# All three mixer gates as seven half-sized products with tokens as the stationary side, in a decoder layer on one core

## The chip, the core and the metric

One core of a Trainium2 chip runs the whole kernel as one program. A core has a matrix engine (TensorE, PE in the profile, its weight loads PEld), a vector engine (VectorE, DVE), a scalar engine (ScalarE, ACT), GpSimd (POOL), a queue engine that issues transfers (SyncE, SP), and 16 DMA engines that all queues share. Each engine works through its own queue in order; semaphores hold an instruction until what it needs is there. The metric is device time in microseconds (us), lower is better.

## What is computed

One layer of a hybrid decoder on 512 tokens of width 1024. The part that matters here is the mixer:

```python
proj = x @ w_in
(da_q, da_k, da_v, sb_q, sb_k, sb_v, dl_q, dl_k, dl_v, gates) = jnp.split(proj, _split_points(), axis=-1)
...
g = jax.nn.sigmoid(gates).reshape(B, S, N_BRANCHES, D)
merged = (g[:, :, 0] * (o_da @ w_branch_da) + g[:, :, 1] * (o_sb @ w_branch_sb)
          + g[:, :, 2] * (o_dl @ w_branch_dil))
return merged @ w_out
```

`o_da`, `o_sb` and `o_dl` are the outputs of differential attention (4 heads), stick-breaking attention (8 heads) and dilated attention (4 heads in 3 groups); each is 512 tokens by 512. The three gates are 512 by 1024 each, so their weights are 1024 by 1024. Behind the mixer come a layer norm, a squared-ReLU MLP, a second sigmoid gate on an embedding, and a second layer norm.

All values are float32. A product is made in three passes of a reduced-precision format: an operand is split into a high part (a cast, on ACT) and a low part (the subtraction, on DVE), and high x high, high x low and low x high add up in PSUM. So each 128x128 block of a product costs three matmuls, and each weight tile costs one cast and one subtraction of 1024 columns.

## The kernel before, in words

The program is a list of *items* made ahead of time; an item is a run of matmuls into one PSUM bank, with an evacuation behind it. The main loop (L1783) goes through the list. For each item it splits the weights that it needs and some ahead, evacuates the item before, takes a step of the attention work, and issues the item's matmuls. A plain input tile (`t_item`, L258) takes another step halfway. A scheduler then orders each engine's instructions by a model of time, so an engine's order is near the program's but not the same.

**Weights.** `load` and `fill` (L165) put 512 KB transfers on SP's queue into seven raw buffers; `split_next` (L200) splits a chunk into one of six pairs of buffers for high and low parts. Weights are thus split up to six chunks, and loaded up to thirteen, ahead of their use.

**Attention.** Each head (or, for differential attention, each head and block of 128 queries) is a generator whose steps are taken by `step` (L1754), started in a fixed order, eight stick-breaking heads, four dilated heads, sixteen differential blocks, under a budget of PSUM banks. Its matmuls, exponentials and copies fall between the items. The order of the input projections is written out in `main_order` (L36): the last ones are the q and k tiles of differential attention, with its value projection after the second head, and eight plain tiles of gate 1.

**Seven products.** Several large products are made by a scheme with seven half-sized products in place of eight (halves of the contraction, tokens and columns), with sums of operand blocks on both sides and sums of the results. The token side is formed once by `mixer_forms` (L515) from a second copy of x that POOL's queue reloads (`load_xr`, L330); products are numbered 1 to 7 after their token form. The weight sums are made in one of two ways: by DVE in the kernel's buffers, or by transfers that copy and accumulate from DRAM to DRAM on POOL's queue (`sum_steps`, L905), eight 512 KB steps per group of four sums, four groups in turn, so many steps per item (`RATES`, L1777). A step waits for a recent subtraction on DVE, so that the transfers spread over the main stream, and for the steps of its own group that it reads.

**Gates and branches.** Gate 1 is eight plain tiles (128 output columns stationary, 512 tokens moving, 24 matmuls each). Gates 2 and 0 are eight *pairs* of column tiles (`gate_pair`, L570), each seven products with a 128-column weight form stationary and 256 tokens moving, 84 matmuls 256 wide. Their weight sums are made by DVE: four additions of 512 columns per pair. Branch tiles (`branch_item`, L545; 12 matmuls 512 wide, weights stationary) are placed between the parts of the pairs. `gate_sig` (L503) applies the sigmoid, behind the last exponential of attention. Products and merged rows have channels on partitions, so the merged tiles are split and used directly as the stationary side of the output projection (`wout_items`, L724).

The value projection of two dilated groups (`value_pair`, L401) and the gate after the mixer (`pleg_items`, L813) are seven-product stages of the other shape: a token form of 128 tokens stationary, 512 weight columns moving, 7 x 2 halves x 12 matmuls.

The lines that pace all this before:

```python
        RATES = 1.8, 1.0
        ...
            if 12 <= n < wout_at - 6:
                credit += it["size"] * (RATES[0] if n < pairs_at[0] else RATES[1])
            elif n > wout_at + 22:
                credit += 1 / 3
```

Of the kernel before, what the change touches and what calls it, by code (L numbers as in the profile page):

```python
# [10 lines left out]
F32 = mybir.dt.float32  # L11
# [24 lines left out]
def main_order():  # L36


    o = [("T", "sb_q", 0), ("T", "sb_k", 0), ("T", "sb_q", 1), ("T", "sb_k", 1), ("V", "sb_v", 0)]
    for j in (2, 3):  # L40
        o += [("T", "sb_q", j), ("T", "sb_k", j)]
    for h in range(4):
        for g in range(3):
            o += [("T", "dl_q", 4 * g + h), ("T", "dl_k", 4 * g + h)]
            if h == 1 and g == 0:
                o += [("V", "dl_v", g)]
        if h == 2:
            o += [("V", "dl_v", 1), ("V", "dl_v", 2)]
    for h in range(4):
        o += [("T", "da_q", h), ("T", "da_k", h)]  # L50
        if h == 1:
            o += [("V", "da_v", 0)]
    for j in range(8):
        o += [("T", "gate", 8 + j)]
    return o


def trunk(tc, a, out):
    nc = tc.nc
    es = ExitStack()  # L60
    with es:
# [210 lines left out]
        def t_evac(name, j):  # L272
            def ev(ps):
# [5 lines left out]
                elif name == "gate":  # L279
                    t = slot("graw")  # L280
                    cp(t, ps)
                    gate_raw[j] = (t, 1.0)
# [199 lines left out]
        for kind, name, j in order[2:]:  # L482
            if kind == "T":
                if name == "gate":
                    continue
# [17 lines left out]
        def gate_sig(i, j):  # L503
            t, sign = gate_raw.pop(8 * i + j)

            with tc.issue_after(last_exp[0]):
                nc.scalar.activation(t, t, AF.Sigmoid, scale=sign)
            sg[i, j] = t
# [36 lines left out]
        def branch_item(i, j):  # L545
            if j % 2 == 0:
                branch_chunk[i] = chunk(a["wb"][i, j // 2].rearrange("p j k m -> p (j k m)"), 1024)
            c = branch_chunk[i]

            def mm(ps):  # L550
                for k in range(4):
                    s = slice(((j % 2) * 4 + k) * P, ((j % 2) * 4 + k) * P + P)
                    h, lo = oTs[4 * i + k]
                    mm3(ps, c["h"][:, s], c["l"][:, s], h, lo, k == 0, k == 3)

            def ev(ps):
                gate_sig(i, j)
                g = sg.pop((i, j))
                nc.vector.tensor_mul(g, g, ps)
                if i == 1:  # L560
                    merged[j] = g
                else:
                    nc.vector.tensor_add(merged[j], merged[j], g)
                if i == 0:
                    merged[j] = split(merged[j], "m")
            item([c] if j % 2 else [], mm, ev, need=[c], size=0.5)

        branch_chunk = {}

        def gate_pair(n, between):  # L570

            i, q = (2, 0)[n // 4], n % 4
            wa, wb = [load(a["wgp"][n, m].rearrange("p b k n -> p (b k n)"), 1024) for m in range(2)]
            ws = load(None, 1024)
            lo, up = slice(0, 512), slice(512, 1024)
            cs = {}
            b = {}

            def first_sums():
                nc.vector.tensor_add(ws["raw"][:, lo], wa["raw"][:, lo], wb["raw"][:, up])  # L580
                nc.vector.tensor_add(ws["raw"][:, up], wb["raw"][:, lo], wb["raw"][:, up])

            def second_sum():
                nc.vector.tensor_add(wb["raw"][:, up], ws["raw"][:, up], wa["raw"][:, lo])

            def third_sum():
                nc.vector.tensor_add(wa["raw"][:, up], wb["raw"][:, up], wa["raw"][:, up])

            def prod(ps, p, start, stop):
                c, o = cs[p]  # L590
                for k in range(4):
                    s = slice(o + k * P, o + k * P + P)
                    mm3(ps, c["h"][:, s], c["l"][:, s], *xf[p][k], start and k == 0, stop and k == 3)

            def bank(name):
                def f():
                    b[name] = at_bank()
                    return b[name]
                return f

            def part_a():
                c = part_of(wa, 0, 1024)
                cs[1], cs[2] = (c, 0), (c, 512)

                def mm(ps):
                    prod(ps[:, HC], 2, True, True)
                    b["s"] = slot("up")
                    nc.scalar.copy(b["s"][:, HB], ps[:, HC])
                    prod(ps[:, HB], 1, True, False)

                def ev(ps):
                    b[0], b[1] = slot("graw"), slot("graw")
                    gate_raw[8 * i + 2 * q], gate_raw[8 * i + 2 * q + 1] = (b[0], 1.0), (b[1], -1.0)
                    nc.vector.tensor_add(b[0][:, HB], ps[:, HB], b["s"][:, HB])
                item([c], mm, ev, need=[c], bank=bank("x"), size=0.5)

            def part_b():
                c3 = part_of(ws, 0, 1024, first_sums, (wa, wb))
                c4 = part_of(wb, 0, 1024, second_sum, (wa, ws))
                cs[7], cs[5], cs[4], cs[6] = (c3, 0), (c3, 512), (c4, 0), (c4, 512)  # L620

                def mm(ps):
                    prod(ps[:, HB], 7, True, False)
                    prod(b["x"][:, HB], 6, False, False)

                def ev(ps):
                    nc.scalar.copy(b["s"][:, HC], b["x"][:, HB])
                    nc.scalar.copy(b["s"][:, HB], ps[:, HB])
                item([], mm, ev, need=[c3, c4], bank=bank("y"), size=0.5)

            def part_c():
                c5 = part_of(wa, 512, 512, third_sum, (wb,))
                cs[3] = (c5, 0)

                def mm(ps):
                    prod(ps[:, HB], 5, False, False)

                def ev(ps):
                    nc.vector.tensor_add(b[1][:, HC], ps[:, HB], b["s"][:, HB])
                item([cs[5][0]], mm, ev, need=[cs[5][0]], bank=lambda: b["x"], size=0.25)  # L640

            def part_e():
                need = [cs[3][0], cs[4][0]]

                def mm(ps):
                    prod(b["x"][:, HB], 3, False, True)
                    prod(ps[:, HB], 4, False, True)

                def ev(ps):
                    nc.vector.tensor_add(b[1][:, HB], ps[:, HB], b["s"][:, HC])  # L650
                    nc.scalar.copy(b[0][:, HC], b["x"][:, HB])
                item(need, mm, ev, need=need, bank=lambda: b["y"], size=0.5)
            part_a()
            for t in between[:2]:
                branch_item(*t)
            part_b()
            for t in between[2:]:
                branch_item(*t)
# [1317 lines left out]
```

## Time and profile before

| | |
|---|---|
| median of three runs | 1056.42 us (1056.42 to 1056.5) |
| span of the profiled execution | 1054.8 us |
| granted TensorE clock | 0.997 |
| instructions | 15599 |

By the trace, the eight plain gate tiles start after the last q and k tiles of differential attention; the gate pairs begin at 479.55 us, the output projection at 629.98 and the embedding gate's products at 688. In the profile, a row of a group names the line, engine, operation, output and inputs with shapes and the count, then the busy time and the mean duration of one, and last the idle time of that engine before them with what ended it. Matmuls are pipelined and their ends are modelled, so a matmul's duration is longer than the time until the next one starts. A row of windows gives the busy time of each engine in a stretch of the span.

### The profile page before, as it was taken

The numbers are of one execution on the slowest core, as the hardware profiler recorded it, in microseconds if no ns is written. First come the engines' busy times: TensorE is split into PE (matmuls) and PEld (weight loads), VectorE is DVE, ScalarE is ACT, GpSimd is POOL, SyncE is SP. The second block draws the span as 40 slices with busy tenths as digits, with TensorE's granted clock in tenths as the row PEclk, the third lists the DMA queues.
The fourth block names the chain that finished last, engine by engine and source line by source line (L and its number), as shares of the span: only waits on it lengthen the run. The fifth ranks groups of instructions, "written<-read, shape, count | busy, mean of one in ns | idle before, by whom it ended". The sixth has DMA issues, their size and how long they took to land.

```text
span 1054.8 us, 15599 instructions
## 1 busy us (share of the span) xinstructions
PE 1044.2 (99%) x5802; PEld 902.9 (86%) x5802; DVE 775.2 (73%) x1386; ACT 571.2 (54%) x994; POOL 145.4 (14%) x223
## 2 busy tenths in 40 slices
PE   9999999999999999999999999999999999999996
PEld 6887788889888888889898988888999889889885
DVE  6888667768764757769768773888777877877966
ACT  6666545536442545547544452685656665666651
POOL 0002401221211102231111130100101100000000
PEclk9999999999999999999999999999999999999998
DMA  8346776976997719872666693258888868777502
GB/s 318 113 151 223 169 208 173 300 271 165 325 310 210 222 39 290 230 240 94 220 173 213 162 334 104 65 160 277 237 298 263 238 243 274 242 236 237 192 34 80
DMA packets 63261, 219.75 MB, mean 208 GB/s; under 512 B 7913, under 2 KB 8825, under 8 KB 63185
## 3 DMA queue, kind: packets, MB, share of 16 engines
q1 hardware_dynamic: 37056, 126.80, 34.6%
q0 software_dynamic: 25552, 91.04, 32.9%
q8 instruction: 45, 0.74, 0.3%
q10 hardware_dynamic: 576, 0.92, 0.2%
q14 instruction: 32, 0.25, 0.1%
HBM read 216.61 MB, written 81.81 MB: 283 GB/s over the span
## 4 chain that ended last, share of the span: by engine, by line
PE 96%; DVE 2%; DMA 0%; ACT 0%; issue 0%; SPq 0%; DVEq 0%
PE mm L89 14%; PE mm L90 13%; PE mm L91 13%; PE at L89 4%; PE at L1094 4%; PE at L1095 4%; PE at L1096 4%; PE at L91 4%; PE at L90 4%; PE mm L458 2%; PE mm L460 2%; PE mm L459 2%; PE at L734 1%; PE at L735 1%; PE at L736 1%; PE at L862 1%
## 5 line engine op out<-in xcount | busy, mean ns | idle before, releaser
L214 ACT CAST wh<-raw 128x1024 fp32r<-128x1024 f32 x249 | 257.2, 1037 | 254.2 <-PE mm L90 146.8
L216 DVE TENSOR_TENSOR wl<-raw,wh 128x1024 fp32r<-128x1024 f32 x249 | 298.7, 1205 | 100.1 <-ACT wh L214 97.4
L89 PE MATMUL mm<-xhT,wh 128*128 128x512 f32 x368 | 147.1, 400 | 0.0
L91 PE MATMUL mm<-xhT,wl 128*128 128x512 f32 x368 | 144.3, 392 | 0.0
L90 PE MATMUL mm<-xlT,wh 128*128 128x512 f32 x368 | 144.0, 391 | 0.0
L91 PEld LDWEIGHTS mm<-xhT,wl 128*128 128x128 f32 x368 | 69.1, 188 | 14.8
L89 PEld LDWEIGHTS mm<-xhT,wh 128*128 128x128 f32 x368 | 69.3, 188 | 13.5 <-issue 0.4
L90 PEld LDWEIGHTS mm<-xlT,wh 128*128 128x128 f32 x368 | 69.2, 188 | 12.7
L1094 PE MATMUL at<-wh,hh 128*128 128x512 f32 x188 | 73.7, 392 | 0.0
L1095 PE MATMUL at<-wl,hh 128*128 128x512 f32 x188 | 73.7, 392 | 0.0
L89 PE MATMUL mm<-x1hT,wh 128*128 128x256 f32 x256 | 73.7, 288 | 0.1
L1096 PE MATMUL at<-wh,hl 128*128 128x512 f32 x188 | 73.1, 389 | 0.0
L90 PE MATMUL mm<-x1lT,wh 128*128 128x256 f32 x256 | 72.2, 283 | 0.0
L91 PE MATMUL mm<-x1hT,wl 128*128 128x256 f32 x256 | 71.8, 283 | 0.0
L89 PEld LDWEIGHTS mm<-x1hT,wh 128*128 128x128 f32 x256 | 48.8, 190 | 4.7 <-ACT up L1028 3.0
L90 PEld LDWEIGHTS mm<-x1lT,wh 128*128 128x128 f32 x256 | 48.9, 191 | 1.5
L932 POOL DMA_DIRECT2D usum<-in_wu_dram x32 | 28.7, 896 | 149.6 <-DVE wl L216 134.6
L91 PEld LDWEIGHTS mm<-x1hT,wl 128*128 128x128 f32 x256 | 48.6, 191 | 0.0
L932 POOL DMA_DIRECT2D dsum<-in_wd_dram x28 | 25.1, 897 | 124.3 <-DVE wl L216 109.2
L1096 PEld LDWEIGHTS at<-wh,hl 128*128 128x128 f32 x188 | 35.3, 188 | 7.7
L1094 PEld LDWEIGHTS at<-wh,hh 128*128 128x128 f32 x188 | 35.5, 189 | 6.0
L1095 PEld LDWEIGHTS at<-wl,hh 128*128 128x128 f32 x188 | 35.5, 189 | 5.5
(521 smaller groups left out, 2663.5 us busy)
## 6 DMA issues: line engine op xcount, KB each, us to landing
usum<-in_wu_dram POOLq DMA_DIRECT2D x48, 512.0 KB, 8.0
raw<-in_wt_dram SPq DMA_DIRECT2D x46, 512.0 KB, 6.3
dsum<-in_wd_dram POOLq DMA_DIRECT2D x42, 512.0 KB, 8.9
raw<-usum SPq DMA_DIRECT2D x32, 512.0 KB, 5.1
raw<-dsum SPq DMA_DIRECT2D x28, 512.0 KB, 4.7
raw<-in_wd_dram SPq DMA_DIRECT2D x25, 512.0 KB, 4.5
raw<-in_wu_dram SPq DMA_DIRECT2D x24, 512.0 KB, 5.0
raw<-in_wv_dram SPq DMA_DIRECT2D x18, 512.0 KB, 8.2
```

What stands on the lines that cost most here:

```text
L89: nc.tensor.matmul(ps, wh, xh, start=start, stop=False, skip_group_check=True)
L90: nc.tensor.matmul(ps, wh, xl, start=False, stop=False, skip_group_check=True)
L91: nc.tensor.matmul(ps, wl, xh, start=False, stop=stop, skip_group_check=True)
L214: i = nc.scalar.copy(h, raw)
L216: i = nc.vector.tensor_sub(lo, raw, h.bitcast(F32))
L458: nc.tensor.matmul(ps, x1, c["h"][:, s], start=k == 0, stop=False)
L459: nc.tensor.matmul(ps, x1, c["l"][:, s], start=False, stop=False)
L460: nc.tensor.matmul(ps, x2, c["h"][:, s], start=False, stop=k == 7)
L932: i = nc.gpsimd.dma_start(o, i, accum_op=OP.add, max_dma_last_dim=4096)
L1094: nc.tensor.matmul(ps, h[:, q], c["h"][:, s], start=go, stop=False, skip_group_check=True)
L1095: nc.tensor.matmul(ps, h[:, q], c["l"][:, s], start=False, stop=False, skip_group_check=True)
L1096: nc.tensor.matmul(ps, lo[:, q], c["h"][:, s], start=False, stop=end, skip_group_check=True)
```

## The change

- All three gates are made by one function, `seven`, in the shape with tokens stationary: 14 items of 12 matmuls per gate. Gate 1 keeps its partial results in SBUF and takes few banks (`gate_alone`), since attention still runs beside it; gates 2 and 0 accumulate in six banks (`gate_chain`).
- The sums of the gates' weights come from DRAM (`msum`, three gates x two halves of the columns' chunks), by more steps of `sum_steps`; the rates of these steps change.
- Branches follow each gate as eight items of 12 matmuls, tokens stationary (`branch_items`). So gates, branches and merged rows have tokens on partitions.
- The merged rows are turned by PE (`turn_item`, 8 x 4 transposes of 128x128), and their split moves behind that. The first half of the output projection is cut in two parts, with the turns of the last four between.
- The value projection and heads 0 and 1 of differential attention move ahead of the last dilated head.

```diff
@@ main_order
-            o += [("V", "dl_v", 1), ("V", "dl_v", 2)]
-    for h in range(4):
-        o += [("T", "da_q", h), ("T", "da_k", h)]
-        if h == 1:
-            o += [("V", "da_v", 0)]
-    for j in range(8):
-        o += [("T", "gate", 8 + j)]
+            o += [("V", "dl_v", 1), ("V", "dl_v", 2), ("V", "da_v", 0)]
+            for d in range(2):
+                o += [("T", "da_q", d), ("T", "da_k", d)]
+    for d in range(2, 4):
+        o += [("T", "da_q", d), ("T", "da_k", d)]
...
-        def branch_item(i, j):
...
-        def gate_pair(n, between):
...
+        def seven(forms, operand, bank_of, done):
+            cs = {}
+            for p in (2, 1, 7, 6, 4, 5, 3):
+                for r in range(2):
+                    if not r:
+                        cs[p] = [operand(p, kp) for kp in range(2)]
+                    def mm(ps, p=p, r=r):
+                        q = slice(r * P, r * P + P)
+                        for k in range(4):
+                            c = cs[p][k // 2]
+                            n = slice(k % 2 * 512, k % 2 * 512 + 512)
+                            h, lo = forms[p][k]
+                            go, end = k == 0 and p in bank_of["first"], k == 3 and p in bank_of["last"]
+                            nc.tensor.matmul(ps, h[:, q], c["h"][:, n], start=go, stop=False, skip_group_check=True)
+                            nc.tensor.matmul(ps, h[:, q], c["l"][:, n], start=False, stop=False, skip_group_check=True)
+                            nc.tensor.matmul(ps, lo[:, q], c["h"][:, n], start=False, stop=end, skip_group_check=True)
...
+        def mixer_operand(n):
+            def f(p, kp):
+                blk = {1: 0, 2: 1, 4: 3}.get(p)
+                return chunk(msum[n][kp][{5: 0, 6: 1, 7: 2, 3: 3}[p]] if blk is None else
+                             a["wgm"][n, kp, blk].rearrange("p k n -> p (k n)"), 1024)
...
+        def branch_items(i, behind=()):
+            for half in range(2):
+                cs = [chunk(a["wb"][i, half, c].rearrange("p k n -> p (k n)"), 1024) for c in range(2)]
+                for tt in range(4):
...
+                    def ev(ps, tt=tt, half=half):
+                        g = sg.pop((i, tt, half))
+                        nc.vector.tensor_mul(g, g, ps)
+                        if i == 1:
+                            merged[tt, half] = g
+                        else:
+                            nc.vector.tensor_add(merged[tt, half], merged[tt, half], g)
...
+        def turn_item(k):
             def mm(ps):
+                for tt in range(4):
+                    nc.tensor.transpose(ps[:, tt * P:tt * P + P], merged[tt, k // 4][:, k % 4 * P:k % 4 * P + P], ident)
             def ev(ps):
+                h, lo = slot("mh", F32R), slot("ml", F32R)
+                nc.scalar.copy(h, ps)
+                nc.vector.tensor_sub(lo, ps, h.bitcast(F32))
+                merged_T[k] = (h, lo)
...
+        gate_alone(0, 1)
+        branch_at = {1: len(items)}
+        branch_items(1)
+        for n, i in ((1, 2), (2, 0)):
+            gate_chain(n, i)
+            branch_at[i] = len(items)
+            branch_items(i, () if i else [lambda k=k: turn_item(k) for k in range(4)])
...
@@ sum_steps
+            todo.extend(up_steps(msum[n][m], a["wgm"][n, m]) for n in range(3) for m in range(2))
             todo.extend(up_steps(gsum[m], a["wg"][m]) for m in range(2))
...
@@ order of attention
-        for hd in range(4):
-            waiting.append((3, dil_head(hd), DIL_PERIOD))
...
+        for kind, hd in (("dl", 0), ("dl", 1), ("dl", 2), ("da", 0), ("da", 1), ("dl", 3), ("da", 2), ("da", 3)):
...
@@ main loop
-        DA_TABS = 47
+        DA_TABS = 44
-        RATES = 1.8, 1.0
+        RATES = 2.6, 1.4
...
-            if n == pairs_at[0] + 3:
+            if n == branch_at[1] - 1:
                 while active or waiting:
                     step()
...
-                credit += it["size"] * (RATES[0] if n < pairs_at[0] else RATES[1])
-            elif n > wout_at + 22:
-                credit += 1 / 3
+                credit += it["size"] * (RATES[0] if n < last_plain else RATES[1])
+            elif n > ple_at + 14:
+                credit += 0.42
...
+            for j in (n, n + 1):
+                if j < len(items) and items[j].get("pre"):
+                    items[j].pop("pre")()
```

The items of the attention stage count from the start of the list: the first gate product is item 65 after the change (the first pair was item 73 before), and `branch_at[1] - 1`, where all attention that is left is stepped through, is item 78 (76 before). `pre` is the sigmoid of a branch tile.

More of the change, by code (lines that the diff above doesn't have):

```diff
@@ L278, in ev @@
                     T[name, j] = evac_twice(ps, name, sc)
[L279 to L282, printed above, removed]
                 else:
@@ L558, in ev @@
[L558 to L568, printed above, removed]
-        def gate_pair(n, between):
[L572 to L658, printed above, removed]
-            part_c()
-            part_e()
@@ L747, in ev @@
                             pending.append(ln1_gen(tt))
-                    item(cs if tt == 3 else [], mm, ev, need=cs, bank=at_bank)
+                    need = [cs[c] for c in sorted({k // 2 for k in ks})]
+                    item(need if last else [], mm, ev, need=need, bank=bank, size=len(ks) / 8)
+                if half:
+                    for tt in range(4):
+                        part(tt, range(8), tt == 3)
+                    continue
+                for tt in range(4):
+                    part(tt, range(4), tt == 3)
+                    for k in {1: (4, 5), 2: (6, 7)}.get(tt, ()):
+                        turn_item(k)
+                for tt in range(4):
+                    part(tt, range(4, 8), tt == 3)
         def ln1_gen(tt):
@@ L1261, in trunk @@
         wout_items()
+        ple_at = len(items)
         ple_items()
@@ L1783, in trunk @@
         for n, it in enumerate(items):
-            if n == last_plain - 1:
-                while any(k not in ready for k in range(4, 8)):
-                    step()
-                split_oT(1)
             if n == v_from[0]:
```

173 lines of the change are left out of this document (118 added, 55 removed).

## The prediction

> **What bounds the kernel now.** I read the page's busy shares first, then its slices, then the chain that ended last.
>
> ```profile
> span 1054.8 us, 15599 instructions
> ...
> PE 1044.2 (99%) x5802; PEld 902.9 (86%) x5802; DVE 775.2 (73%) x1386; ACT 571.2 (54%) x994; POOL 145.4 (14%) x223
> ...
> PEclk9999999999999999999999999999999999999998
> DMA  8346776976997719872666693258888868777502
> PE 96%; DVE 2%; DMA 0%; ACT 0%; issue 0%; SPq 0%; DVEq 0%
> q1 hardware_dynamic: 37056, 126.80, 34.6%
> q0 software_dynamic: 25552, 91.04, 32.9%
> ...
> PE 96%; DVE 2%; DMA 0%; ACT 0%; issue 0%; SPq 0%; DVEq 0%
> ```
>
> TensorE is busy 99% of the span at full clock, and 96% of the chain is its own work. There is hardly a gap to win back: the time is the number of matmuls times the pace at which they start. A busy PE alone would not prove that, since matmul ends are modelled, so the pace comes from stages that hold one kind of matmul. The DMA line has slices at 9 beside slices at 1 to 3; I come back to it.
>
> Stages, by windows: us, then busy time and instruction count of PE, PEld, DVE, ACT, POOL, the clock, the DMA share and GB/s.
>
> ```profile
> 688.20:726.50 38.30, 38.30 (x168) 31.47 (x169) 35.16 (x47) 27.98 (x43) 1.63 (x3) 1.00 0.61 201
> 734.32:747.32 13.00, 13.00 (x110) 12.94 (x109) 7.33 (x10) 9.58 (x16) 1.70 (x2) 1.00 0.95 267
> 479.55:629.98 150.43, 150.43 (x976) 136.06 (x975) 116.32 (x165) 76.57 (x124) 23.28 (x36) 1.00 0.66 200
> 238.31:281.60 43.29, 43.29 (x205) 38.92 (x204) 37.33 (x88) 23.09 (x42) 9.66 (x14) 1.00 0.81 211
> 170.85:238.31 67.46, 67.46 (x322) 56.26 (x322) 46.06 (x76) 30.99 (x48) 15.86 (x26) 1.00 0.91 281
> ```
>
> The first is the sigmoid gate after the mixer, seven products with the token forms stationary and 512 weight columns moving: 168 matmuls in 38.30 us, 228 ns each. The second holds only 256-wide matmuls, from the MLP's up part: 13.00 us over 109 weight loads, 119 ns each, more than half of 228. The third is all eight gate pairs with their 24 branch tiles. The fourth is the seven-product value pair with attention mixed in, the fifth ten input tiles.
>
> **Part 1: the gate products, before.** Gate 1 was eight plain tiles of 24 matmuls 512 wide, 192 in all: 192 x 228 ns = 43.8 us. The other gates were eight pairs of 84 matmuls 256 wide; a third of them shows in these groups, the branches' third in the last:
>
> ```profile
> L89 PE MATMUL at<-xhT,wh 128*128 128x256 f32 x128 | 37.6, 294 | 0.0
> L89 PE MATMUL at<-u4h,wh 128*128 128x256 f32 x32 | 9.1, 285 | 0.0
> L89 PE MATMUL at<-u7h,wh 128*128 128x256 f32 x32 | 9.1, 284 | 0.0
> L89 PE MATMUL at<-u6h,wh 128*128 128x256 f32 x32 | 9.1, 283 | 0.0
> L89 PE MATMUL mm<-oTh,wh 128*128 128x512 f32 x96 | 37.6, 392 | 0.0
> ```
>
> 3 x (128 + 96) = 672. (The means include the modelled tail, so they are not the pace.) At 119 ns they take 80.0 us. From their own stage they take more: 150.43 us less 288 branch matmuls at 228 ns (65.7) and 16 small ones of attention at 0.11 (1.8) leaves 82.9 us, 123 ns each; the difference holds that stage's small waits. So before: 123.8 to 126.7 us.
>
> **Part 2: the gate products, after.** Three gates, each 7 products x 2 token halves x 12 matmuls, 512 wide: 504 x 228 = 114.9 us. The trace has this very form (38.30 us a gate, with all evacuations), so this is well known. Branches stay 288 matmuls 512 wide, tokens now stationary: no change. The output projection keeps 192.
>
> **Part 3: the transposes.** 8 x 4 of 128x128 are new. The nearest row, from the chain of waits, has 128-wide fp32 work:
>
> ```profile
> 289.34 1.78 PE at L1634 x16
> ```
>
> 0.11 us each, so 32 take 3.6 us, all on PE. The copy and the subtraction behind each group replace, one for one, the splits of the merged tiles that existed; the turns of 4 to 7 stand between output-projection parts of 2.7 us each, which cover their evacuation.
>
> Sum on PE: 114.9 + 3.6 - (123.8 to 126.7) = **-5.3 to -8.2 us**. I take -6.5: the lower end assumes that the new gates wait as much as the pairs did, the upper that they wait not at all.
>
> The skill speaks against the size of this. The Trainium skill, TensorE: Matmul & The Clock Gate, Back-to-back issue gap, gives N/2.4 + 2.5 ns, an estimate of 109 ns at 256 and 216 at 512: almost no loss in narrow matmuls, and the sum would be -4.2 us. The rows (119 and 228) say that narrow ones lose more, and the trace decides.
>
> **Part 4: ACT and DVE.** Per 1024 columns of weights one cast and one subtraction; per pair four 512-wide weight sums (L580 and three like it):
>
> ```profile
> L214 ACT CAST wh<-raw 128x1024 fp32r<-128x1024 f32 x249 | 257.2, 1037 | 254.2 <-PE mm L90 146.8 <-PE at L90 42.6 <-PE at L1096 17.4
> L216 DVE TENSOR_TENSOR wl<-raw,wh 128x1024 fp32r<-128x1024 f32 x249 | 298.7, 1205 | 100.1 <-ACT wh L214 97.4 <-PE at L1576 1.5
> L580 DVE TENSOR_TENSOR raw<-raw,raw 128x512 f32<-128x512 f32 x8 | 5.5, 687 | 0.1
> L614 DVE TENSOR_TENSOR graw<-at,up 128x256 f32<-128x256 f32 x8 | 3.4, 420 | 0.2 <-PE at L91 0.2
> L507 ACT ACTIVATE graw<-graw 128x512 f32<-128x512 f32 x24 | 14.5, 629 | 0.3 <-DVE graw L650 0.3
> ```
>
> Splits go from 8 + 8 x 3.5 = 36 to 42: +6.2 us ACT, +7.2 DVE. The 32 weight sums leave: -22 us DVE. Evacuations on DVE go from 24 of 256 columns (10.1 us) to 24 of 512 (16.5). DVE gets some 8 us lighter, ACT some 8 heavier; the seven-product row (35.16 of 38.30 us DVE, 27.98 ACT, PE never idle) shows that their load hides behind PE. Sigmoids stay 24 and are only issued up to two items earlier, behind the last exponential. I cost this at nothing. If the cover goes, a half product waits for its bank, some 0.7 us at a time.
>
> **Part 5: DMAs.** Loads for the gates go from 8 + 16 = 24 to 42 of 512 KB, sums on the POOL queue grow by 6 groups of 8, 152 to 200. By the queue rows q1 takes 0.346 x 1054.8 / (126.80 / 0.524) = 1.51 us of all 16 engines per load, q0 0.329 x 1054.8 / (91.04 / 0.524) = 2.0 us per sum. That is +27 + 96 = 123 us on 712: 68% becomes 80%. No transfer is on the chain now. In a gate stage, 14 loads (21.1) and 14 x 0.5 x 1.4 = 9.8 sums (19.6) ask for 40.7 us in 38.3; its branch stage asks for 4 x 1.51 + 5.6 x 2.0 = 17 in 8 x 2.74 = 22; together 58 of 60 us. Seven raw buffers and six split ones run ahead, about 13 chunks of 2.7 us, so an excess of 2.4 us is absorbed. I take nothing; bounds: a gain excluded, a loss up to the excess itself, 3 x 2.4 = 7 us.
>
> **Part 6: order and rates.** The value projection and heads 0 and 1 of differential attention move ahead of the last dilated head; the matmuls are the same. Differential attention was covered by eight plain gate tiles (43.8 us, two steps each) and two more items; now by 13 half products (35.6 us, one step each), and by my count of the steps some eight are left and forced at once before the last half product. What they issue (transposes, a copy, the value product, square, power, multiplication, transposes, a copy) is a chain of eight, from 0.28 to 1.05 us each by the groups below and the power's further down, some 6 us with a hop of 0.1 to 0.2 between each:
>
> ```profile
> L1580 ACT ACTIVATE scr<-at 128x128 f32<-128x128 f32 x16 | 4.5, 278 | 14.1 <-PE at L1576 14.0
> ...
> L1597 ACT ACTIVATE oT<-at,gcol 128x512 f32<-128x512 f32 x4 | 2.7, 685 | 5.9 <-PE at L1595 5.9
> ```
>
> The last half product and the first branch tiles (2.7 us each) do not need that chain and can run in it. I take 0.5 us; bounds 0 (nothing excludes full cover) and 6. The queue that all this passes is POOL's: the power (L1586) and the reloads of x (L353, L337) stand in order behind sums that wait for earlier sums.
>
> Sum: -6.5 + 0.5 = -6.0, span 1048.8 us. The median, 1056.42, is 1.6 above the profiled span; so **1050.4 us**.
>
> **Rival 1, slower: POOL's queue runs late.** Here is its busiest stretch (start, duration, what, and the idle time before it), first and last of nine, then the reload of x; then the power's group; then two windows:
>
> ```profile
> 172.77 0.88 POOL L932 DMA_DIRECT2D gsum<-in_wg_dram  x1 [2.24 <-DMA gsum<-gsum]
> ...
> 196.24 0.81 POOL L932 DMA_DIRECT2D gsum<-in_wg_dram  x1 [0.27 <-DMA gsum<-gsum]
> ...
> 214.29 1.10 POOL L353 DMA_DIRECT2D xr<-in_xT_dram  x2 [5.74 <-DVE wl L216]
> ```
>
> ```profile
> L1586 POOL TENSOR_TENSOR ms<-ms,mhalf 128x4 f32<-128x4 f32 x4 | 4.2, 1046 | 16.7 <-DVE ms L1585 12.0 <-DVE rr L1555 4.7
> ```
>
> ```profile
> 180.00:200.00 20.00, 20.00 (x101) 16.57 (x100) 13.20 (x24) 10.04 (x16) 4.97 (x7) 1.00 1.00 294
> ...
> 260.00:280.00 20.00, 20.00 (x97) 17.27 (x96) 18.60 (x30) 9.07 (x12) 6.67 (x10) 1.00 1.06 280
> ```
>
> Eight issues in 23.5 us is 0.34 per us, with the engines full. At 2.6 sums per item of 6.75 us (67.46 / 10) the demand becomes 0.385. From item 12 to the first gate 46 x 2.6 = 120 sums and 53 loads ask for 320 us in some 335. The queue may thus fall behind, by 0.045 x 67 = 3 sums or 9 us in that stage. What speaks against it: POOL had caught up before the reload (it waited 5.74 us for DVE) and before all four powers; a sum may be issued once the split four chunks back has run, about three items or 20 us ahead of what has to follow in time. If the lag passes 20 us and reaches some 35, the multiplication behind the power, or the first form of x, holds DVE; two matmul banks cover one item (7 us), and PE loses about 35 - 20 - 7 = 8 us, at two places: 1050.4 + 16 = **1066 us**. The Trainium skill bears on it: DMA: Bandwidth & Descriptors, Issuing engines are not separate DMA queues, says that transfers of all issuing engines run on the same 16 engines and interleave; the two windows at full share agree.
>
> **Rival 2: the gates' loads come late.** The excess of part 5 isn't absorbed since both queues share the engines: +7 us, **1057.4 us**, no change. For it: 0.61 share in the seven-product row without sums beside it. Against: PE lost nothing in the 260 to 280 window at full share, inside the value pair.
>
> **Rival 3: the attention tail stands bare.** +6 for the forced steps: **1056.4 us**.
>
> **How the numbers follow.** Forecast 0.57, alone 1047.5 to 1053.5 (all of part 1's wait won back; the forced steps half bare). Rival 1 0.20, rival 2 0.10, rival 3 0.05, rivals together or a wait that I don't see 0.08. A measurement here tells 0.2%, 2.1 us, from no change. Faster: the forecast, 0.57. Same: rivals 2 and 3, 0.15. Slower: the rest, 0.28. Range 1047 to 1066: it leaves out a rival 1 dearer than worked out, and a gain past 9 us.
>
> **What would show it.** Right: three gate stages of 38 to 39 us at 228 ns, no 256-wide matmul on x, transposes at 0.11, a branch stage of 22 us, PE still 99%, powers that wait for DVE and not behind sums. Wrong: DVE idle behind POOL's power or a reload; matmuls waiting for a split that waited for a load; a gap of some us before the first branch tile; or 512-wide matmuls of the gates over 235 ns each.

## The result, and the profile after

The changed kernel takes 1071.94 us (median of four runs, 1070.18 to 1073.48) against 1056.42: a ratio of 1.0147, 95% interval 1.0133 to 1.0162. It is slower by 1.5%, where 1050.4 and faster was forecast, and above the range's end of 1066. The page of its profiled execution, by the lines that were shown of before:

```profile
span 1071.8 us, 15018 instructions
...
PE 1046.1 (98%) x5474; PEld 889.5 (83%) x5474; DVE 764.1 (71%) x1352; ACT 576.8 (54%) x982; POOL 179.5 (17%) x271
...
PEclk9999999998999999898999999999999999999999
DMA  8348987998999999387599993248999879857612
...
q0 software_dynamic: 32464, 116.21, 41.1%
q1 hardware_dynamic: 39648, 136.24, 36.4%
...
PE 82%; DMA 10%; DVE 5%; issue 1%; ACT 1%; POOL 0%; DVEq 0%; SPq 0%; POOLq 0%; ACTq 0%
```

PE is still 98% busy, and from that one share nobody would find 17 us. Two other lines show it. The chain that ended last was 96% PE before; now 10% of it are transfers and 5% DVE. And the clock line, full up to the last slice before, has an 8 in three slices in the middle. Windows show what was made well and where it went wrong (the columns are those of the prediction's windows: us, PE, PEld, DVE, ACT, POOL, clock, DMA share, GB/s):

```profile
523.53:561.61 38.08, 38.08 (x170) 31.53 (x168) 23.52 (x26) 24.79 (x32) 8.15 (x11) 1.00 0.97 257
561.61:583.37 21.76, 21.76 (x98) 18.02 (x96) 14.20 (x19) 5.35 (x6) 2.96 (x4) 1.00 1.03 339
583.37:621.45 38.08, 38.08 (x170) 31.53 (x168) 24.08 (x27) 24.80 (x32) 9.44 (x15) 1.00 0.95 287
234.00:252.00 18.00, 13.71 (x60) 11.55 (x59) 12.19 (x25) 4.97 (x7) 5.57 (x8) 0.81 1.04 289
440.00:455.00 15.00, 11.56 (x51) 9.40 (x50) 14.81 (x32) 9.85 (x23) 0.52 (x1) 0.83 0.18 47
488.00:506.00 18.00, 13.27 (x50) 10.42 (x49) 9.50 (x14) 9.98 (x17) 3.44 (x6) 0.72 0.82 294
```

The first three rows are gate 2, its branch and gate 0: 38.08, 21.76 and 38.08 us with PE never idle. (Fences show excerpts of a view; "..." stands for rows left out.) The new work costs what the forecast said. The last three are three short stretches, one in the value pair (A), one in the first gate's early products (B), one just before the first branch tile (C). In each PE loses 3.4 to 4.7 us outright and the clock falls to 0.72 to 0.83. PE's own list of waits between 225 and 506 us (line waited for, us in total, times, longest) names them:

```profile
PE mm L420 <- ACT dl_q L285: 4.3, 1, 4.3
PE at L1600 <- DVE lg L1595: 3.4, 2, 2.9
PE at L1633 <- DVE on L1627: 2.7, 1, 2.7
PE at L1614 <- DVE wT L98: 2.1, 1, 2.1
```

**A, at 239 us.** The first row names ACT, but ACT is only the last link. DVE's list of waits between 225 and 262 us, and POOL's timeline before it (start, duration, what, idle time before it and what ended it), tell what was late:

```profile
DVE fr L370 <- DMA xr<-in_xT_dram: 10.5, 1, 10.5
```

```profile
210.04 0.53 POOL L970 DMA_DIRECT2D msum<-msum  x1 [3.42 <-DMA msum<-in_wgm_dram]
...
216.09 0.52 POOL L970 DMA_DIRECT2D msum<-msum  x1 [3.20 <-DMA msum<-in_wgm_dram]
218.85 0.56 POOL L347 DMA_DIRECT2D xr<-in_xT_dram  x1 [2.25 <-DMA msum<-in_wgm_dram]
...
230.26 0.54 POOL L347 DMA_DIRECT2D xr<-in_xT_dram  x1 [0.72 <-DMA msum<-msum]
...
235.47 0.54 POOL L347 DMA_DIRECT2D xr<-in_xT_dram  x1 [1.68 <-DMA msum<-msum]
```

The eight reloads of x stand one behind the other on POOL's queue, behind the last sum at 216.09, and still take 16.6 us to go out: the first at 218.85, the last at 235.47. Before, all of them went between 214.29 and 218.03. What each waits for is in the trace's semaphore records: the transfers of this queue carry eight semaphores in rotation, and a transfer goes out only when the one eight places ahead of it, which used the same semaphore, has landed. The eight sums ahead of the reloads were issued from 198.04 to 216.09 and took 18.8 to 25.0 us to land (DMA share 1.04 from 198 to 236 us); each reload went out 0.3 to 0.6 us behind the landing of its one. Before, the transfers eight places ahead landed in 7.5 to 12.8 us and had been there for 1.8 to 14.3 us. Over the whole run, 68 of POOL's 250 transfers went out less than 0.7 us behind that landing; before it was 17 of 202.

The chain of waits between 225 and 262 us leads from there to PE, and shows PE's pace behind the gap:

```profile
210.04 20.21 DMA msum<-msum
230.26 7.93 DMA xr<-in_xT_dram
...
240.29 1.14 DVE fr L370 x2
...
241.98 1.04 ACT wh L212
243.04 0.61 ACT dl_q L285
243.69 0.82 PE mm L420
244.51 0.43 PE mm L421
...
251.53 0.24 PE at L420
```

The view draws the copy from 210.04 to the next issue, 20.21 us; by its semaphore it landed after 21.5. The reload of 230.26 landed 7.93 us later. DVE makes the token sums of the value pair from the reloads (L370). ACT casts them, and behind these casts, in ACT's order, stands the copy (L285) that empties the bank of PE's next product: it ends at 243.65, and PE starts at 243.69. So PE did not wait for the forms themselves but for a bank whose copy stood behind them. Then read the matmuls: 0.43 us from one to the next for about 7 us, 0.24 after that. Those are the same instructions at half clock.

**B, at 447 us.** PE's last matmul of product 2 started at 447.22. The next thing in PE's order are attention's transposes (L1600), and then DVE's timeline beside that wait:

```profile
450.55 1.11 PE L1600 MATMUL at<-ident,lg 128*128 128x128 f32 x4 [2.94 <-DVE lg L1595]
```

```profile
447.42 0.17 DVE L1592 RECIPROCAL rr<-ss 128x2 f32<-128x2 f32 x1
447.49 0.68 DVE L522 SCALAR_TENSOR_TENSOR xr<-xr,xr 128x512 f32<-128x512 f32 x1
448.08 0.16 DVE L1593 TENSOR_TENSOR rr<-rr,lam 128x1 f32<-128x1 f32 x1
448.15 0.69 DVE L530 TENSOR_TENSOR xlT<-xr,xhT 128x512 fp32r<-128x512 f32 x1
448.75 0.49 DVE L1594 TENSOR_SCALAR lg<-lg,rr 128x512 f32<-128x512 f32 x1
449.14 0.69 DVE L238 TENSOR_TENSOR u6l<-xr,u6h 128x512 fp32r<-128x512 f32 x1
449.75 0.75 DVE L1595 SCALAR_TENSOR_TENSOR lg<-lg,rr,lg 128x512 f32<-128x512 f32 x1
```

PE waits for the last of these rows, which ends at 450.50. Between the steps of that block (L1592 to L1595) stand the subtractions of the token forms (L522, L530, L238), 2.1 us in these rows. DVE is busy 14.81 of the 15.00 us of the window above, so there was no room for both.

**C, at 491 to 499 us.** This is the end of differential attention: weights copied by DVE (L98), value product (L1614), square, power on POOL, multiplication (L1627), transposes (L1633), each waiting for the one before, 2.2 and 3.0 us of PE idle in two places. Here the forced steps stand.

**Where 17 us of span came from.** The change has 312 matmuls 512 wide more, 672 of 256 columns fewer and 32 of 128 more. At the trace's own paces from start to start (0.227, 0.120 and 0.110 us) that is +70.8 - 80.6 + 3.5 = -6.3 us. Gaps over 0.45 us after the first 20 us of the span (from one start to the next, less the pace) sum to 0 before and 16.4 after: 13.5 at A, B and C, and two of 1.8 and 1.1 us at 307 and 360 us. 512-wide matmuls at 0.427 us, half clock, cost 5.4 us more than before. Sum: -6.3 + 16.4 + 5.4 = 15.5 of 17.0; the other 1.5 us are the balance of narrower matmuls at half clock (3.2 us) and smaller delays elsewhere (1.7 us less than before).

### The profile page after: what moved, and what is told of

Its sections match the earlier page's. It is cut to its first block, busy times and chain, and to the rows that moved or that the text cites. A ratio compares the mean times of both kernels' runs of the same rounds, so it can differ in the third digit from the quotient of the medians.

```text
span 1071.8 us, 15018 instructions
## 1 busy us (share of the span) xinstructions
PE 1046.1 (98%) x5474; PEld 889.5 (83%) x5474; DVE 764.1 (71%) x1352; ACT 576.8 (54%) x982; POOL 179.5 (17%) x271
## 3 DMA queue, kind: packets, MB, share of 16 engines
q0 software_dynamic: 32464, 116.21, 41.1%
q1 hardware_dynamic: 39648, 136.24, 36.4%
## 4 chain that ended last, share of the span: by engine, by line
PE 82%; DMA 10%; DVE 5%; issue 1%; ACT 1%; POOL 0%; DVEq 0%; SPq 0%; POOLq 0%; ACTq 0%
PE mm L87 8%; PE mm L89 8%; PE mm L88 8%; PE at L1131 4%; PE at L1132 4%; PE at L1133 4%; DMA msum<-in_wgm_dram 4%; PE at L552 3%; PE at L553 3%; PE at L554 3%; PE at L645 2%; PE at L646 2%; PE at L647 2%; DMA msum<-msum 2%; PE mm L452 2%; PE mm L454 2%
## 5 line engine op out<-in xcount | busy, mean ns | idle before, releaser
L214 DVE TENSOR_TENSOR wl<-raw,wh 128x1024 fp32r<-128x1024 f32 x251 | 305.5, 1223 | 135.8 <-ACT wh L212 133.6
L212 ACT CAST wh<-raw 128x1024 fp32r<-128x1024 f32 x251 | 263.3, 1051 | 253.9 <-PE mm L88 123.5
L87 PE MATMUL mm<-xhT,wh 128*128 128x512 f32 x304 | 121.1, 398 | 1.0 <-DVE da_qb L101 1.0
L89 PE MATMUL mm<-xhT,wl 128*128 128x512 f32 x304 | 119.2, 392 | 0.1
L88 PE MATMUL mm<-xlT,wh 128*128 128x512 f32 x304 | 118.9, 391 | 0.0
L87 PEld LDWEIGHTS mm<-xhT,wh 128*128 128x128 f32 x304 | 57.2, 188 | 12.7 <-PE at L1600 1.2
L89 PEld LDWEIGHTS mm<-xhT,wl 128*128 128x128 f32 x304 | 57.1, 188 | 12.6 <-DVE wl L214 0.5
L88 PEld LDWEIGHTS mm<-xlT,wh 128*128 128x128 f32 x304 | 57.1, 188 | 10.4
```

The source lines that it names most:

```text
L87: nc.tensor.matmul(ps, wh, xh, start=start, stop=False, skip_group_check=True)
L88: nc.tensor.matmul(ps, wh, xl, start=False, stop=False, skip_group_check=True)
L89: nc.tensor.matmul(ps, wl, xh, start=False, stop=stop, skip_group_check=True)
L212: i = nc.scalar.copy(h, raw)
L214: i = nc.vector.tensor_sub(lo, raw, h.bitcast(F32))
```

## The experiments

Before ran beside every one, with medians of 1056.17 to 1056.36 us. Where a run's edit takes several lines, its core is shown.

**The new rates in the kernel before.** Nothing else of the change.

```diff
-        RATES = 1.8, 1.0
+        RATES = 2.6, 1.4
```

> The kernel before, with the rates of the changed one (2.6 and 1.4 sums per item); all 152 sums run, only earlier. Theory A (POOL's queue of sums makes the reload of x for the value products late, DVE waits 10.5 us, PE stands 4.5 us and loses its clock for 6.8 us): the first stall appears here too, near 239 us, and the time is 1056.4 + 4.5 + 3.4 = about 1064 us. Rival (the stall needs the gate sums or the new order of attention): the reload stays on time, 1055 to 1058 us.

Measured: 1064.29 us, ratio 1.0071 (1.0056 to 1.0086). DVE's and PE's waits, then POOL's first and last reload, of that run:

```profile
DVE fr L376 <- DMA xr<-in_xT_dram: 9.8, 1, 9.8
```

```profile
PE mm L426 <- ACT dl_q L291: 3.6, 1, 3.6
```

```profile
217.34 0.56 POOL L353 DMA_DIRECT2D xr<-in_xT_dram  x1 [2.59 <-DMA usum<-in_wu_dram]
...
233.06 0.54 POOL L353 DMA_DIRECT2D xr<-in_xT_dram  x1 [0.84 <-DMA dsum<-dsum]
```

Stall A without any of the new gates: what is in the queue are sums for the MLP. So the rate alone costs 8 us by the medians (5.6 in the profiled execution, the fastest of the four: a gap of 3.9 us and 1.4 us of half clock), and the new sums are only what filled the rate. Here too every reload goes out 0.3 to 0.6 us behind the landing of the sum eight places ahead.

**The change without the gates' sums.** The 48 transfers are gone and the rates are the old ones.

```diff
-            todo.extend(up_steps(msum[n][m], a["wgm"][n, m]) for n in range(3) for m in range(2))
...
-                return chunk(msum[n][kp][{5: 0, 6: 1, 7: 2, 3: 3}[p]] if blk is None else
-                             a["wgm"][n, kp, blk].rearrange("p k n -> p (k n)"), 1024)
+                return chunk(a["wgm"][n, kp, 2 if blk is None else blk].rearrange("p k n -> p (k n)"), 1024)
...
-        RATES = 2.6, 1.4
+        RATES = 1.8, 1.0
```

> The changed kernel without the 48 transfers of the gates' weight sums and with rates 1.8 and 1.0; the four summed weight forms of each gate are replaced by a stored block, so the gates' values are not the reference's, with the same loads, splits and matmuls. If all three large stalls (at 239, 447 and 491 us) come from the DMA traffic, all go: 1072 - 26 = about 1046 us. If theory A holds for the first alone and the other two come from attention packed beside the first gate, only the first goes: 1072 - 8 = about 1064 us, with stalls of about 3 and 5 us left before and at the end of the first gate.

Measured: 1061.6 us (1.0056; 1.0039 to 1.0073). A is gone, 10 us of the loss with it. B (3.1 us) and C (2.2 and 3.2 us) stand as they were, so they are no matter of transfers.

**The reload of x earlier.** It is allowed to start four items sooner.

```diff
-            v_from[0] = len(items) - 4
+            v_from[0] = len(items) - 8
...
-        WAIT = 5
+        WAIT = 13
```

> The changed kernel with the reload of x for the value products issued four items earlier, the forms made at the same steps. Theory A: DVE no longer waits for the reload, the stall at 239 us and the half-clock stretch behind it go, 1072 - 8 = about 1064 us; the other two stay. Rival (engines simply full there, the wait moves to another transfer): 1070 to 1073 us.

Measured: 1068.39 us (1.0111; 1.0096 to 1.0126), 3.6 below the change and not 8. A is gone, but a gap of 2.0 us opens at 295.7. DVE's waits of this run between 280 and 305 us:

```profile
DVE shf L1374 <- DMA sh<-rv: 5.2, 3, 4.2
```

The next user of POOL's queue, the position tables of differential attention, now comes out late: its four transfers go out at 279.55 to 286.98, each 0.5 to 0.6 us behind the landing eight places ahead. The lateness was handed on, half clock included. Neither expectation gave this time: theory A was right about the stall and did not see the next one.

**No forced steps before the branches.** Only heads that haven't started are stepped; the last ones run at their own pace under the branch tiles.

```diff
-                while active or waiting:
+                while waiting:
                     step()
```

> The changed kernel without the forced steps of attention before the last half product of the first gate: the steps go on, one per branch tile. Theory C (the last differential block's chain stands bare there: 2.2 and 3.0 us, then 10.2 us at half clock): both gaps and the half-clock stretch go, 1072 - 10 = about 1062 us. Rival (PE stands there because the branch weights or the split of the attention output are late): the gap stays, 1069 to 1073 us.

Measured: 1060.77 us (1.0041; 1.0026 to 1.0056), 11.2 below the change. The window of stall C in this run, beside the row above:

```profile
488.00:506.00 18.00, 18.00 (x88) 15.04 (x87) 11.62 (x16) 9.39 (x16) 3.12 (x5) 1.00 0.82 303
```

PE is never idle there, clock 1.00, and 88 matmuls start where 50 did. A and B stand.

**Token forms two items later.** Two more pauses between the seventh and sixth form, so that their work doesn't stand ahead of attention's on DVE and of product 2's copies on ACT.

```diff
             form(xf, 7, r22)
             yield
             yield
+            yield
+            yield
```

> The changed kernel with the second token form (for products 6, 5 and 4) made two steps later. Theory B (the copy that frees the first gate's PSUM bank stands on ACT behind the casts of this form, which wait for DVE, so PE has no product to make at 447 us): the stalls of 0.7 and 3.1 us and the half-clock stretch behind them go, 1072 - 7 = about 1065 us. Rival (the wait is for the differential block's own row of DVE work, which would be as late): the stall stays within 0.5 us, 1070 to 1073 us.

Measured: 1068.51 us (1.0116; 1.0101 to 1.0131), 3.4 below the change and not 7. The gap of 3.1 us is gone; 0.6 stays of B and a new one of 1.4 us stands at 461, where attention's next scores wait for DVE. C's two gaps grew from 5.2 to 6.2 us. So the forms' work at that place is the cause of B, and taking it away is worth half of what was expected. The expectation puts the wait on ACT's copies. The edit moves the forms on both engines, so the run can't tell them apart; the row of PE's wait above does, and it names DVE.

**Reloads, tables and tail together.** The third and fourth run's edits, and the position tables fetched six items earlier.

```diff
-            if n == DA_TABS:
+            if n == DA_TABS - 6:
```

> Early reload of x, the position tables for differential attention fetched six items earlier (turned at the same item), and no forced steps. In the run with the early reload alone DVE waited 4.25 us for these tables at 293 us. Theory A (what POOL's queue brings late is what stalls): no stall is left before 350 us nor at the end of the first gate: only the one at 440 us, about 1060.8 - 8 = 1052 us. Rival (the lateness passes on to the next transfer on POOL's queue each time): another stall of 2 us or more before 430 us, 1056 us or more.

Measured: 1055.74 us (0.9999; 0.9987 to 1.001). Of the three stalls only B is left, 3.1 us with half clock behind it. That is 3.7 us above what was expected, and not to be told from the kernel before.

**All four mends.** The run before with the later forms as well; the edits are those shown.

> The same with the second token form two steps later. If the sum on the matrix engine (-5.3 to -8.2 us) was right and the stalls are all that was missing: no stall over 2 us, clock full throughout, 1047 to 1051 us, faster than the kernel before. Rival (small waits from full DMA engines are spread through the stages): 1053 us or more with no large stall.

Measured: 1053.95 us (0.9981; 0.9971 to 0.999). Full clock throughout and no gap over 1.4 us, yet 3.5 us above the forecast: the rival's sign.

**All four, without the gates' sums.** To see whether the rest is traffic.

> The four mends together (earlier reload of x, earlier position tables, no forced steps, later token forms), without the 48 transfers of the gate weights' sums and at the old rates 1.8 and 1.0; the summed forms are replaced by a stored block, so the gates' values are not the reference's. It asks what the last 3 us between the version with four mends (1053.95) and the forecast (1050.4) are. Theory A, full DMA engines: the small waits come from late loads and late POOL work, so without the sums it falls to 1047 to 1050. Rival, the attention work packed into a shorter stage with fewer steps: it stays at 1052 to 1054, with the same gaps of about 1 us at the places where attention and the gate products meet.

Measured: 1052.25 us (0.9961; 0.9947 to 0.9975), in the rival's range and with the rival's gaps: 1.1, 0.6 and 1.4 us at 351, 436 and 454, all where PE waits for DVE's part of attention. Theory A's 1047 to 1050 did not come. Traffic is worth 1.7 us by the medians, and the two intervals overlap a little (0.9947 to 0.9975, and 0.9971 to 0.999 with the sums).

**All four, with the sums elsewhere.** Two places were tried. First the stage between output projection and embedding gate, where the DMA line shows 2 to 4:

```diff
-        RATES = 2.6, 1.4
+        RATES = 2.1, 1.4
...
-            elif n > ple_at + 14:
-                credit += 0.42
+            elif n > wout_at + 2:
+                credit += 1.0 if n <= ple_at + 14 else 0.42
```

> The four mends with the right values, but with the transfers of sums moved out of the attention stage: rate 2.1 in place of 2.6 there, 1.4 as before, and 1.0 from the output projection to the embedding gate, where the DMA share falls to 2 and 5 tenths. If full DMA engines cost the last 3 us: 1050 to 1052.5 us. If attention's packing does, no change from 1053.95. If sums in the layer norm's stage hold POOL's work there, a new gap of some us near 640 to 690 us and 1054 to 1058.

Measured: 1061.53 us (1.0045; 1.003 to 1.006), more than any of the theories expected. The attention stage is as in the run without sums, but DVE's waits between 640 and 690 us and POOL's timeline say:

```profile
DVE xn L724 <- POOL lr L718: 8.7, 2, 8.1
```

```profile
659.75 0.53 POOL L972 DMA_DIRECT2D dsum<-dsum  x1 [4.74 <-DMA dsum<-in_wd_dram]
662.96 0.52 POOL L972 DMA_DIRECT2D usum<-usum  x1 [2.67 <-DMA usum<-in_wu_dram]
665.80 0.52 POOL L972 DMA_DIRECT2D dsum<-dsum  x1 [2.33 <-DMA dsum<-in_wd_dram]
666.33 0.59 POOL L718 TENSOR_TENSOR lr<-lr,mhalf 128x1 f32<-128x1 f32 x1
```

The layer norm's power, 0.59 us of work, stands behind sums that each wait for an earlier one of their own group; the transfers eight places ahead had landed 7 us and more before. The share of the 16 engines from 630 to 690 us was 0.28 with all four mends and is 0.82 here: the engines had room, the queue had not. Then the MLP's stage:

```diff
-        RATES = 2.6, 1.4
+        RATES = 2.0, 1.4
...
-                credit += 0.42
+                credit += 0.8
```

> The four mends, with rate 2.0 in the attention stage in place of 2.6 and 0.8 in place of 0.42 in the MLP's, so the same 200 sums later. If full DMA engines in the attention stage cost the last 3 us: 1050 to 1053 us, unless the MLP's loads, which already fill 8 to 9 tenths of the engines, come late: then gaps behind 750 us and 1055 to 1060. If attention's packing does, 1054.

Measured: 1066.42 us (1.0094; 1.0079 to 1.0109). The MLP's window with rate 0.8, then the same window with rate 0.42 (all four mends):

```profile
760.00:900.00 140.00, 132.34 (x853) 120.31 (x852) 99.14 (x127) 79.64 (x121) 28.44 (x42) 0.98 1.04 335
```

```profile
760.00:900.00 140.00, 140.00 (x926) 128.05 (x926) 107.78 (x139) 85.50 (x132) 15.86 (x24) 1.00 0.90 280
```

At a share of 0.90 nothing waits; with 18 more instructions on POOL, at 1.04, PE loses 7.7 us in the window and 2.6 just before it, half clock apart. PE's waits there are for copies on ACT (L1067, L1082), and in the chain of waits before the first gap of the window the cast ahead of such a copy waits for a load of summed weights that took 19.61 us to land. So the loads come late under full engines, as the expectation's "unless" has it, at more than its price.

**All four, rates shifted a little.** 2.4, 1.6 and 0.43, then 2.2, 1.8 and 0.45, from 2.6, 1.4 and 0.42.

```diff
-        RATES = 2.6, 1.4
+        RATES = 2.2, 1.8
...
-                credit += 0.42
+                credit += 0.45
```

> The four mends with rates 2.4, 1.6 and 0.43: half as far. If the small waits near 383 and 413 us of the version with four mends come from the engines being full, half of them go: 1052.5 to 1053.5 us. If any stage is tipped over by 0.2 more per item: 1055 or more.

> The four mends with rates 2.2, 1.8 and 0.45 in place of 2.6, 1.4 and 0.42: fewer sums in the attention stage, more in the gate stages. If the engines hold 0.89 to 0.92 in the gate stages at rate 1.4, 0.4 per item more asks for about 0.1 more there, so they are full but not over. If that still fits: 1052 to 1053 us. If a gate stage then waits for its loads, one gap of 2 to 4 us with half clock behind it: 1056 to 1060.

Measured: 1053.34 us (0.9975; 0.9965 to 0.9985) and **1052.15 us** (0.996; 0.9945 to 0.9975; four runs, 1051.78 to 1052.35). Both are where they were expected. The second is as fast as the version without the gates' sums (1052.25), so at these rates the 48 transfers cost nothing that shows; 35 of POOL's 250 transfers go out right behind the landing eight places ahead, 70 at 2.6 and 1.4. It is the best of several rates tried, with four runs against ten of all four mends (1052.16 to 1056.39), and the two intervals overlap a little. It beats both kernels: 0.4% below before, 1.8% below the change. Its PE waits between 200 and 960 us:

```profile
PE at L131 <- DVE mx L1585: 1.2, 1, 1.2
PE mm L87 <- DVE da_qb L101: 1.0, 1, 1.0
PE at L1602 <- DVE lg L1597: 0.5, 1, 0.5
...
```

## Why the prediction was wrong, and where it was right

**Parts 1 to 3, PE's own work: right.** -6.5 us was taken; the counts at the trace's paces give -6.3. A gate takes 38.08 us (38 to 39), a branch 21.76 (22), and four transposes take 0.44 us, 0.11 each, in the chain of waits of after:

```profile
641.73 0.44 PE mm L669 x4
```

The sum by the formula of the Trainium skill, TensorE: Matmul & The Clock Gate, Back-to-back issue gap, was -4.2; the trace does not agree with it (0.227, 0.120 and 0.110 us). That section of the Trainium skill gives the formula for an isolated matmul, not for a stream with a weight load for each, so it did not speak against the size as the prediction has it.

**Part 5, transfers: the amount right, "I take nothing" right only for the engines.** The sum of 712 + 123 = 835 us of all engines came out at (41.1 + 36.4)% of 1071.8 = 831. The gate stages at shares of 0.95 to 1.03 lose nothing, so rival 2 didn't come. What the part left to the rival is the queue's order.

**Part 6 and rival 1, POOL's queue: the mechanism named, its chance and threshold wrong.** This is the first step that failed: "POOL had caught up before the reload" and a lag of "3 sums or 9 us" that a lead of 20 us absorbs. The lag was worked out as rate against rate. That part stayed small: the first reload went out 4.6 us later than before. But what each reload waits for is the landing of the transfer eight places ahead, and under full engines that took 18.8 to 25.0 us, so the eight took 16.6 us to go out in place of 3.7, and the last was 17.4 us late. Rival 1's price was 8 us a place; measured were +7.9 from the rates alone in the old kernel, -10.3 without sums and with the old rates. That 8 and 7.9 agree is chance: the price was idle time at a lag of 35 us, and what came was a gap of 3.9 us with half clock behind it, at a lag of 17. The second place, the power of differential attention, did not stall PE for this reason: without the sums C's gaps are as long.

**Part 6, the forced steps: 0.5 us taken, bounds 0 to 6, 8.6 measured at the place.** "The last half product and the first branch tiles do not need that chain and can run in it" is the second step that failed. They don't need it, but on PE's queue they stand behind its matmuls. The idle time of 5.2 us lies within the bounds; in the half clock behind it, 10.24 us long, the matmuls come 3.4 us late against their pace. Letting the tail run on under the branches won 11.2 us back. Between the two profiled executions it is 11.5: 5.2 are gaps and 5.2 half clock, of which 1.8 is at A and B, where it was shorter that time.

**Part 4, ACT and DVE: "I cost this at nothing" was wrong by 3.4 us or more.** Their sums are near what was worked out (DVE 11.1 us less against some 8, ACT 5.6 more against some 8). But the first gate's early products stand beside the token forms and attention, and there DVE is busy 14.81 of 15.00 us; the seven-product row that was to show the cover has no attention beside it. One wait of some 0.7 us is there; the other became 3.1, as a block's last step on DVE stood behind the forms' subtractions. The cover named was one stage's average; at that place the order on DVE decided.

**What no part had: the clock.** Each stall was priced at its idle time. Half clock behind three of them added 5.4 us in 512-wide matmuls alone, and 8.6 us over all widths (matmuls started in the three stretches, against their pace): half as much again as the 16.4 us of gaps. And the rivals were weighed one at a time, with 0.08 for several together: here the first place of rival 1, rival 3 and a loss in part 4 came at once, so the time lies past the range's end.

**The forecast as a whole.** With the three stalls out and the sums spread, the new structure takes 1052.15 us, 1.75 above 1050.4 and within the forecast's own range, which is a statement on the mended kernel and not on the change as it was forecast. Gaps of 1.1, 0.6 and 1.4 us that wait for DVE's part of attention are left; they do not move with traffic. Whether another order of attention's steps would remove them was not tried.

## What to carry to other kernels

A busy share and an engine's total say whether work fits; where a stage is tight, the order in each queue says what waits. Before raising the rate of background transfers, list everything else that goes through the queue that issues them (reloads, tables, a small power), look in the trace at which earlier landing each issue waits for, and give each a lead longer than that landing takes under load. Price a stall of 2 us or more on TensorE with the half clock that may follow, and look for idle engines and a free queue both before moving transfers to a quiet stage.

## What the runs showed of the hardware

**The clock after a gap.** Records of granted clock 0.5 in the middle of the runs last 3.41, 6.83 or 10.24 us, that is one, two or three times 3.41. They followed gaps (from one start to the next, less the pace) of 2.0 us (reload earlier, 3.41), 2.3 (sums in the idle stage, 3.41), 3.9 (new rates in before, 3.41), 4.5 (A, 6.83) and the pair of 2.2 and 3.0 (C, 10.24). Not every gap has one: that of 3.1 us in B had 6.83 in the change, 3.41 in the run with the early reload and none in the run without the gates' sums, a gap of 2.4 us in the run with sums in the idle stage had none of its own, and gaps up to 1.8 us had none. The Trainium skill, TensorE: Matmul & The Clock Gate, What's actually happening, gives a free-running window of 3413 ns and a table of two states, full and half rate; lengths and values agree. The same page of the Trainium skill, Why this matters for your kernels, warns of idle gaps over about 3 us; here 2.0 us were enough once, and 3.1 not always, and the measurement decides.

**Landing under full engines, and eight in flight.** Eight copies and sums of 512 KB from DRAM to DRAM in a row took 18.8 to 25.0 us to land at a DMA share of 1.04; in the kernel before, those at the same place took 7.5 to 12.8 us. In these kernels POOL's transfers carry eight semaphores in rotation: in none of the fourteen traces does one go out ahead of the landing eight places before it. So whatever is issued on that queue under such a load, a reload or a table, can stand for one such landing.
